# Tiled fp32 products become one entry of the schedule, and the planner charges tiling changes and strided operands

## The chip, the core and the metric

The kernel runs on one core of a Trainium2 chip. Of the core's engines this case needs TensorE (PE in the profile, with its weight loads apart as PEld), VectorE (DVE), ScalarE (ACT), GpSimd (POOL) and the queue SP that issues the DMAs. All of them run at once and meet at semaphores. The metric is the device time of one execution in microseconds; lower is better.

## The reference, cut to what matters

A two-layer encoder trunk on 512 tokens of width 1024, in float32. Each layer has four token mixers side by side, then a gated MLP with a short convolution:

```
h = rms_norm(x, attn_norm_g[i])
u_s5, conv_in, q_lat, kv_lat, k_pe, q_g, k_g, v_g = split(h @ w_in[i])
y_s5   = s5_mixer(u_s5, ...)        # two-way diagonal complex scan, 16 groups of 16 channels, state 64
y_conv = conformer_conv(conv_in)    # GLU, depthwise conv of 31 taps, LayerNorm, swish
y_mla  = mla_mixer(q_lat, kv_lat, k_pe, ...)   # 4 heads of 64, softmax over 512 keys
y_gqa  = gqa_mixer(q_g, k_g, v_g, ...)         # 4 heads of 64, 2 key/value heads
x = x + rms_norm(stack(y_s5, y_conv, y_mla, y_gqa)) @ w_out[i]
h = rms_norm(x, ffn_norm_g[i])
u = depthwise_conv3(h @ w_up[i]); gate, up = split(u)
x = x + (silu(gate) * up) @ w_down[i]
```

After both layers a last `rms_norm` gives the output.

## The kernel before

Activations lie transposed: channels on the 128 partitions, the 512 tokens along the free axis. Large products are taken in three passes of `fp32r` (a high and a low half of each operand; `mm3`, `product`); small ones are plain `fp32`, which takes two PE instructions for one product. Weights come by DMA, and DVE and ACT split them into halves.

The order of the work is not the order of the code. Every call on `V`, `A`, `T`, `X`, `GP` is put by `add` into a list of operations with their operands, and `_Plan.run` makes a schedule of that list: it walks a model of the five engines (`forward`), gives each operation a cost in ns from `_cost`, a delay between engines from `LAT`, and takes for each idle engine the ready operation of the highest priority whose buffers fit (51 `s` slots, 22 `b` slots, 16 `t` slots in SBUF, and the 8 banks of PSUM). Ten passes (`PASSES`) alternate with a backward walk that sets new priorities; the pass with the shortest model span is kept. `emit` then issues each operation in that order, so each engine's program is a fixed sequence. A copy (`copy`) may go to ACT or DVE; the walk decides. ACT holds one set of function tables at a time, and the walk takes `SWITCH` off the priority of an operation that needs another set.

All instructions are issued from one line of `emit`, L536, and table loads from L534, so the profile's groups have to be read by shape and operand names, not by line. In those names `bank` is a PSUM bank, `v_s`, `v_b`, `v_t` are SBUF slots, `c_sb` holds constants (the identity for transposes, a matrix of ones for sums), `xs__65` is the residual stream.

Four places use PE in column tiles: two or four products with 64 or 32 output columns run side by side in the array, each writing its own partitions of one bank. They go through `plan.tiled`, which takes the list of products of one row of tiles and enters them as one operation (a "group"); its cost is the largest of the row's products plus 53 ns for each further one. Below, "row" is one such set of tiles that run side by side.

- `s5_prep`, the kernel of the scan: 4 rows of two 64-column tiles, 128 moving columns, for each of 4 quarters and 2 layers (32 rows). Layer 1's run beside layer 0's MLP.
- `s5_out`, the output of the scan: 6 rows of the same kind for each of 4 quarters and 2 layers (48 rows).
- `attend`, probabilities times values: 4 rows of two 64-column tiles, 512 moving columns, for each of 4 pairs of heads and 2 layers (32 rows).
- `conv`, the depthwise convolution on PE: 4 rows of four 32-column tiles, 512 moving columns, 2 for each of 3 channel blocks (24 rows).

That is 136 rows, 136 operations, and the walk is free to put any other PE work between two rows. Where it does, PE changes its tiling. `_cost` knows nothing of that.

Of the kernel before, what the change touches and what calls it, by code (L numbers as in the profile page):

```python
# [17 lines left out]
P = 128  # L18
D = 1024
S = 512  # L20
# [91 lines left out]
class _Op:  # L112
    __slots__ = ("idx", "alts", "outs", "ins", "deps", "succ", "ndep", "ready", "rank", "bias", "boost", "eng", "done", "t0", "bufs")
# [9 lines left out]
class _Plan:  # L123
# [49 lines left out]
    def add(self, alts):  # L173
        op = _Op()
        op.idx, op.alts = len(self.ops), alts
# [7 lines left out]
        deps = set()  # L183
# [19 lines left out]
    def tiled(self, mms):  # L203

        d = max(_cost("T", *m)[4] for m in mms) + 53.0 * (len(mms) - 1)
        return self.add([("T", "group", mms, {}, d, 0.0, 0.0)])
# [103 lines left out]
    def forward(self, prio, ref, home, horizon):  # L310
# [9 lines left out]
        n = len(ops)  # L320
# [34 lines left out]
        act_set = self.LOG  # L355
        head = 0
# [46 lines left out]
        while len(order) < n:  # L403
            progress = False
            for e in free:
# [3 lines left out]
                for l in (("V", "F") if e == "V" else (e,)):  # L409
                    tries = 0  # L410
                    for z in cand[l]:
                        k = -z[0]
                        if bk is not None and k <= bk:
                            break
                        if e == "A":
                            st = self.act_of(z[3])
                            if st is not None and act_set not in st:
                                k -= self.SWITCH
                                if bk is not None and k <= bk:
                                    continue  # L420
                        if tries > self.TRIES and z[2] is not ops[ref[head]]:
                            continue
                        got = fits(z[2])
                        if got is not None:
                            best, bk, bg = z, k, got
                        else:
                            tries += 1
# [32 lines left out]
                dur = al[4]  # L460
                if e == "A":
# [41 lines left out]
    LAT = {("A", "V"): 140.0, ("V", "V"): 127.0, ("T", "V"): 196.0, ("T", "A"): 197.0, ("V", "A"): 200.0,  # L503
# [4 lines left out]
    SWITCH = 4000.0  # L508
    BETA = 40.0
# [46 lines left out]

def _cost(e, fn, a, k):
# [9 lines left out]
    elif e == "V":  # L567
# [13 lines left out]
        else:  # L581
            d = 68.0 + 1.04 * n
    elif e == "A":
# [5 lines left out]
        if "accum_out" in k:  # L589
            d += 90.0  # L590
    elif e == "G":
# [8 lines left out]
def trunk_kernel(  # L600
# [167 lines left out]
    def s5_prep(l, bias=0.0):  # L768
# [150 lines left out]
        for q4 in range(4):  # L919
# [38 lines left out]
            for pr in range(2):  # L958
                for c_ in range(2):
                    plan.tiled([("matmul", (kp[64 * e:64 * e + 64, pr], bm[:, c_, 2 * pr + e, :], gri[c_][:, 2 * pr + e]),  # L960
                                 {"start": c_ == 0, "stop": c_ == 1}) for e in range(2)])
# [76 lines left out]
    def s5_out(l, U, st):  # L1038
# [3 lines left out]
        for hf in range(2):  # L1042
            o_, p_ = ps((P, 4, P)), ps((P, 8, NC_))
            for q4 in range(2):
# [6 lines left out]
                for pr in range(2):  # L1051
                    for i in range(3):
                        plan.tiled([("matmul", (
                            o_[64 * e:64 * e + 64, 2 * q4 + pr],
                            U[:, 8 * hf + 4 * q4 + 2 * pr + e, :] if i == 0 else st[hf][:, i - 1, 4 * q4 + 2 * pr + e, :],
                            w_[i][:, 2 * pr + e, :]), {"start": i == 0, "stop": i == 2}) for e in range(2)])
# [59 lines left out]
    def attend(scores, vt):  # L1116
# [22 lines left out]
        for kb in range(4):  # L1139
            plan.tiled([("matmul", (o_[64 * hh:64 * hh + 64], vt[hh][:, kb, :], pt[hh][kb // 2][:, kb % 2, :]),  # L1140
                         {"start": kb == 0, "stop": kb == 3}) for hh in range(2)])
# [29 lines left out]
    def mixing(l):  # L1171
# [174 lines left out]
        def conv():  # L1346
            cv = []
            o, ot = VEC["dw_w"][0], VEC["dw_t"][0]
            for j in range(2):
# [22 lines left out]
                for gg in range(2):  # L1372
# [3 lines left out]
                    for f_ in range(4):  # L1376
                        plan.tiled([("matmul", (p_[32 * i:32 * i + 32], wt[:, 4 * i + f_, gg, :], win[i][:, f_:f_ + S]),
                                     {"start": gg + f_ == 0, "stop": gg + f_ == 4}) for i in range(4)])
# [337 lines left out]
```

## Time and profile before

| what | value |
|---|---|
| device time, median of 3 runs | 1236.8 us (1235.83, 1236.8, 2334.42) |
| device time of the profiled execution | 1235.14 us |
| its span, first to last instruction | 1233.1 us |
| granted TensorE clock, mean | 0.993 |
| instructions | 19808 |
| HBM read and written | 118.96 MB and 13.89 MB, 108 GB/s over the span |

The run at 2334.42 us stands alone; the other two and the profiled one agree within 0.2%. By time the program falls into the mixers of layer 0 (until about 225 us), its MLP (until about 620 us, with the first products of layer 1 in its last part), the mixers of layer 1 (until about 830 us) and its MLP. A busy time of PE in the profile counts a matmul from its start to a modelled end, so PE can be "busy" while its array waits; the starts of the matmuls are what shows its pace.

### The profile page before, as it was taken

The page shows a single profiled execution, that of the slowest core. Times are in us where ns is not written, and L with a number is a line of the kernel's source. Part 1 is how long each engine was busy: PE and PEld are TensorE (multiplying, and loading weights), DVE is VectorE, ACT ScalarE, POOL GpSimd, SP SyncE. Part 2 cuts the span into 40 slices and gives each one's busy share as a digit, 9 for nine tenths or more (in the row PEclk, how much of TensorE's full clock was granted, in tenths as well). Part 3 has the DMA queues.
Part 4 walks back from the last instruction along what each step waited for, and adds up shares of the span by engine and source line. Part 5 has one row for each costly group of instructions (what it writes and reads, how often), then busy time and mean ns, then how long its engine had stood idle before and what let it go on. Part 6 is the DMA issues. An engine that isn't in the chain of part 4 may idle for free.

```text
span 1233.1 us, 19808 instructions
## 1 busy us (share of the span) xinstructions
PE 1193.4 (97%) x7144; PEld 974.5 (79%) x7144; DVE 1122.9 (91%) x2204; ACT 718.1 (58%) x1366; POOL 6.9 (1%) x27
## 2 busy tenths in 40 slices
PE   7999999999999999979999999999999799999996
PEld 5874455778999998968878736558899799999996
DVE  8999988879999999999997997996899998999876
ACT  6348599446647566645463266883656454656543
POOL 0000000000000000000000000000000000000000
PEclk9999999999999999999999999999999999999998
DMA  8469582302333333314584164622124332333202
GB/s 320 137 215 270 118 218 78 112 1 86 103 95 102 105 95 109 98 61 144 188 283 121 35 148 91 181 77 70 46 89 131 94 103 91 107 101 111 89 1 69
DMA packets 88962, 144.64 MB, mean 117 GB/s; under 512 B 22176, under 2 KB 34976, under 8 KB 88736
## 3 DMA queue, kind: packets, MB, share of 16 engines
q1 hardware_dynamic: 88864, 143.38, 38.2%
q8 instruction: 56, 0.92, 0.3%
q14 instruction: 42, 0.34, 0.1%
HBM read 118.96 MB, written 13.89 MB: 108 GB/s over the span
## 4 chain that ended last, share of the span: by engine, by line
PE 77%; DVE 14%; ACT 4%; DMA 2%; issue 2%; SPq 1%; DVEq 0%; ACTq 0%
PE bank L536 77%; DVE v_s L536 11%; ACT v_s L536 3%; DVE v_b L536 2%; ACT v_b L536 1%; DVE v_t L536 1%; SPq L536 1%; DMA v_s<-y_d 0%; DMA v_s<-in_w_up_dram 0%; DMA y_d<-v_b 0%; ACT L534 0%; DMA v_b<-in_w_in_dram 0%; DVE xs__65 L536 0%; DMA v_b<-k_d 0%; DVEq L1711 0%
## 5 line engine op out<-in xcount | busy, mean ns | idle before, releaser
L536 PE MATMUL bank<-v_b,v_s 128*128 128x256 f32 (+3 forms) x3382 | 576.2, 293 | 4.3 <-DVE v_b L536 3.8
L536 PEld LDWEIGHTS bank<-v_b,v_s 128*128 128x128 f32 (+1 forms) x3382 | 478.1, 188 | 29.4 <-issue 7.2
L536 DVE TENSOR_TENSOR v_s<-v_s,v_s 128x512 fp32r<-128x512 f32 (+6 forms) x691 | 431.0, 654 | 12.7 <-ACT v_s L536 7.3
L536 PE MATMUL bank<-v_s,v_s 128*128 128x512 f32 (+2 forms) x1492 | 434.9, 378 | 2.4 <-DVE v_s L536 1.8
L536 PE MATMUL bank<-v_s,v_b 128*128 128x512 f32 (+3 forms) x1465 | 353.6, 416 | 12.1 <-ACT v_b L536 8.3
L536 PEld LDWEIGHTS bank<-v_s,v_s 128*128 128x128 f32 (+1 forms) x1492 | 254.1, 184 | 60.4 <-issue 9.9
L536 PEld LDWEIGHTS bank<-v_s,v_b 128*128 128x128 f32 (+2 forms) x1465 | 221.0, 173 | 94.5 <-issue 33.9
L536 ACT CAST v_s<-v_s 128x512 fp32r<-128x512 f32 (+2 forms) x387 | 224.2, 603 | 106.0 <-DVE v_s L536 77.2
L536 PE MATMUL bank<-v_b,v_b 128*128 128x256 f32 (+6 forms) x365 | 109.4, 408 | 6.7 <-DVE xs__65 L536 5.0
L536 ACT ACTIVATE v_s<-v_s 128x512 f32<-128x512 f32 (+2 forms) x121 | 69.6, 586 | 72.2 <-DVE v_s L536 71.5
L536 ACT ACTIVATE v_s<-bank 128x256 f32<-128x256 f32 x146 | 55.5, 384 | 84.8 <-PE bank L536 82.5
L536 DVE TENSOR_TENSOR xs__65<-xs__65,bank 128x512 f32<-128x512 f32 x120 | 80.4, 681 | 25.8 <-PE bank L536 25.6
L536 DVE SCALAR_TENSOR_TENSOR v_s<-v_s,vec__67,v_s 128x511 f32<-128x511 f32 (+7 forms) x130 | 95.8, 742 | 2.5 <-DMA v_s<-y_d 1.5
L536 PEld LDWEIGHTS bank<-v_b,v_b 128*128 128x128 f32 (+3 forms) x365 | 54.5, 175 | 28.7 <-issue 11.2
L536 DVE TENSOR_TENSOR v_b<-v_b,v_b 128x1024 fp32r<-128x1024 f32 (+5 forms) x74 | 75.7, 1035 | 1.0 <-ACT v_b L536 0.9
L536 ACT CAST v_b<-v_b 128x1024 fp32r<-128x1024 f32 (+3 forms) x57 | 53.6, 948 | 33.9 <-DVE v_b L536 10.4
L536 PEld LDWEIGHTS bank<-c_sb,v_s 128*128 128x128 f32 x360 | 43.5, 142 | 30.0 <-issue 18.1
L536 PE MATMUL bank<-c_sb,v_s 128*128 128x128 f32 x360 | 61.2, 279 | 3.1 <-ACT v_s L536 1.9
L536 ACT ACTIVATE v_s<-v_s,vec__67 128x512 f32<-128x512 f32 x51 | 41.3, 814 | 31.7 <-DVE v_s L536 31.5
L536 DVE TENSOR_TENSOR v_s<-v_b,v_s 128x128 f32<-128x128 f32 (+4 forms) x109 | 54.9, 521 | 2.0 <-ACT v_b L536 1.2
L536 DVE SCALAR_TENSOR_TENSOR v_s<-v_s,nfw__68,v_s 128x511 f32<-128x511 f32 x66 | 49.2, 745 | 3.4 <-ACT v_s L536 3.2
L536 DVE TENSOR_TENSOR v_s<-v_s,bank 128x256 f32<-128x256 f32 x109 | 44.6, 414 | 8.3 <-PE bank L536 7.3
(107 smaller groups left out, 802.0 us busy)
## 6 DMA issues: line engine op xcount, KB each, us to landing
v_s<-in_w_up_dram SPq DMA_DIRECT2D x164, 256.0 KB
v_b<-in_w_in_dram SPq DMA_DIRECT2D x28, 512.0 KB
v_s<-in_w_dn_dram SPq DMA_DIRECT2D x50, 256.0 KB
v_b<-in_w_out_dram SPq DMA_DIRECT2D x16, 384.0 KB
v_b<-v_b SPq DMA_DIRECT2D x24, 256.0 KB
v_s<-x_d SPq DMA_DIRECT2D x21, 257.5 KB
v_s<-in_w_dn_dram SPq DMA_DIRECT2D x26, 192.0 KB
v_s<-wt_d SPq DMA_DIRECT2D x16, 256.0 KB
```

Of the source, the lines that this page charges most:

```text
L536: self.issued(op, getattr(eng[e], fn)(*[res(z) for z in a], **{n: res(z) for n, z in k.items()}))
```

## The change

It has four parts, all in what the planner is told.

1. `tiled` takes a list of rows and enters them as one operation. The loops over rows in `s5_prep`, `s5_out`, `attend` and `conv` become lists handed over in one call, so that the 136 rows are 30 operations: 8 of 4 rows, 8 of 6, 8 of 4 and 6 of 4. Their cost is the sum over rows of the largest product in each; the 53 ns for each further tile are gone. An operation of several rows is placed when the operands of all its rows are ready.
2. The walk keeps the tiling in force on PE (`tiles`). An operation with another tiling loses `RETILE` (1000) of its priority, and is charged 175 ns when it is taken.
3. `_cost` charges a DVE operation of 64 elements and more 0.7 ns for each element if an operand's innermost stride is not 0 or 1 (`_broken`), and an ACT operation 95 ns for such an operand or for an output of under 128 partitions.
4. The delay from DVE to ACT in `LAT` goes from 200 to 130 ns.

What is computed, the buffers and the DMAs stay the same; every engine's order is planned anew.

```diff
-    def tiled(self, mms):
-
-        d = max(_cost("T", *m)[4] for m in mms) + 53.0 * (len(mms) - 1)
-        return self.add([("T", "group", mms, {}, d, 0.0, 0.0)])
+    def tiled(self, rows):
+
+        d = sum(max(_cost("T", *m)[4] for m in mms) for mms in rows)
+        op = self.add([("T", "group", [m for mms in rows for m in mms], {}, d, 0.0, 0.0)])
+        op.tiles = len(rows[0])
+        return op
...
+        tiles = 1
...
+                        if e == "T" and z[2].tiles != tiles:
+                            k -= self.RETILE
+                            if bk is not None and k <= bk:
+                                continue
...
                 dur = al[4]
+                if e == "T" and op.tiles != tiles:
+                    dur += 175.0
+                    tiles = op.tiles
...
-    LAT = {("A", "V"): 140.0, ("V", "V"): 127.0, ("T", "V"): 196.0, ("T", "A"): 197.0, ("V", "A"): 200.0,
+    LAT = {("A", "V"): 140.0, ("V", "V"): 127.0, ("T", "V"): 196.0, ("T", "A"): 197.0, ("V", "A"): 130.0,
...
+    RETILE = 1000.0
...
+def _broken(z):
+
+    if not isinstance(z, _Ap):
+        return False
+    dims = [d for d in list(z.proto.ap)[1:] if d[1] > 1]
+    return bool(dims) and dims[-1][0] not in (0, 1)
...
+        if n >= 64 and any(_broken(z) for z in a):
+            d += 0.7 * n
...
+        if a[0].shape[0] < P or any(_broken(z) for z in a):
+            d += 95.0
...
-            for pr in range(2):
-                for c_ in range(2):
-                    plan.tiled([("matmul", (kp[64 * e:64 * e + 64, pr], bm[:, c_, 2 * pr + e, :], gri[c_][:, 2 * pr + e]),
-                                 {"start": c_ == 0, "stop": c_ == 1}) for e in range(2)])
+            plan.tiled([[("matmul", (kp[64 * e:64 * e + 64, pr], bm[:, c_, 2 * pr + e, :], gri[c_][:, 2 * pr + e]),
+                          {"start": c_ == 0, "stop": c_ == 1}) for e in range(2)] for pr in range(2) for c_ in range(2)])
...
-        for kb in range(4):
-            plan.tiled([("matmul", (o_[64 * hh:64 * hh + 64], vt[hh][:, kb, :], pt[hh][kb // 2][:, kb % 2, :]),
-                         {"start": kb == 0, "stop": kb == 3}) for hh in range(2)])
+        plan.tiled([[("matmul", (o_[64 * hh:64 * hh + 64], vt[hh][:, kb, :], pt[hh][kb // 2][:, kb % 2, :]),
+                      {"start": kb == 0, "stop": kb == 3}) for hh in range(2)] for kb in range(4)])
```

The calls in `s5_out` and `conv` change in the same way. In the changed program the issuing line is L547 and table loads stand at L545.

Three places show what moves. The first is PE in the mixers of layer 0, before: rows of `s5_out` (output `64x128`, one printed row a row of tiles) alternate with products of other work (`128x512`).

```order
L536 MATMUL bank4_76<-v211_s10_1277,v252_b16_1512 64x128 x2
L536 MATMUL bank5_77<-v263_b9_1575,v49_b13_295 128x512
L536 MATMUL bank4_76<-v213_s12_1285,v252_b16_1512 64x128 x2
L536 MATMUL bank5_77<-v250_s33_1502,v61_b21_358 128x512
L536 MATMUL bank4_76<-v216_s43_1300,v83_b12_475 64x128 x2
L536 MATMUL bank0_72<-v267_s11_1599,v74_s32_429 128x512
L536 MATMUL bank4_76<-v211_s10_1277,v252_b16_1512 64x128 x2
L536 MATMUL bank2_74<-v238_b4_1450,v243_s16_1474 128x512
L536 MATMUL bank4_76<-v213_s12_1285,v252_b16_1512 64x128 x2
L536 MATMUL bank0_72<-v253_s30_1514,v81_s36_466 128x512
```

The same work on PE in the changed program:

```order
L547 MATMUL bank5_77<-v214_b8_1265,v223_s8_1326 128x512
L547 MATMUL bank1_73<-v237_s7_1432,v88_b17_521 64x128 x2
L547 MATMUL bank1_73<-v233_s44_1420,v270_b0_1602 64x128 x2
L547 MATMUL bank1_73<-v218_s18_1297,v270_b0_1602 64x128 x2
L547 MATMUL bank1_73<-v237_s7_1432,v88_b17_521 64x128 x2
L547 MATMUL bank1_73<-v233_s44_1420,v270_b0_1602 64x128 x2
L547 MATMUL bank1_73<-v218_s18_1297,v270_b0_1602 64x128 x2
L547 MATMUL bank3_75<-c_sb_63,v263_s38_1575 128x128
```

Six rows stand behind each other, with a change of tiling ahead and one behind, where before each row had both.

The second place is PE in the first attention of layer 0, before: the rows of `attend` (output `64x512`, two printed rows a row of tiles) have transposes (`c_sb`) or other products between them.

```order
L536 MATMUL bank2_74<-v338_b17_1876,v258_s47_1545 64x512
L536 MATMUL bank2_74<-v355_b14_1939,v258_s47_1545 64x512
L536 MATMUL bank3_75<-c_sb_63,v346_s21_1904 128x128
L536 MATMUL bank2_74<-v338_b17_1876,v258_s47_1545 64x512
L536 MATMUL bank2_74<-v355_b14_1939,v258_s47_1545 64x512
L536 MATMUL bank3_75<-c_sb_63,v346_s21_1904 128x128
L536 MATMUL bank2_74<-v339_b6_1881,v258_s47_1545 64x512
L536 MATMUL bank2_74<-v358_b7_1951,v258_s47_1545 64x512
L536 MATMUL bank0_72<-v290_b19_1687,v279_b1_1648 128x512
```

And in the changed program:

```order
L547 MATMUL bank7_79<-v307_b2_1753,v311_b16_1766 128x512
L547 MATMUL bank1_73<-v325_b0_1857,v242_s39_1468 64x512
L547 MATMUL bank1_73<-v328_b9_1863,v242_s39_1468 64x512
L547 MATMUL bank1_73<-v325_b0_1857,v242_s39_1468 64x512
L547 MATMUL bank1_73<-v328_b9_1863,v242_s39_1468 64x512
L547 MATMUL bank1_73<-v329_b15_1867,v242_s39_1468 64x512
L547 MATMUL bank1_73<-v336_b1_1895,v242_s39_1468 64x512
L547 MATMUL bank1_73<-v329_b15_1867,v242_s39_1468 64x512
L547 MATMUL bank1_73<-v336_b1_1895,v242_s39_1468 64x512
L547 MATMUL bank3_75<-v339_s28_1919,c_sb_63 128x512
```

The transposes that stood between the rows have gone ahead of them or behind them.

The third place is ACT near the end of the attention of layer 0, before: the last loads of function tables there stand three operations apart, around one tanh (`v8_t4_148` is its bias) and one swish (`vec__67`).

```order
L536 ACTIVATE v443_s49_2269,v392_t3_2077<-bank4_76,v438_t1_2243 128x512
L534 ACT_TABLE_LOAD
L536 ACTIVATE v445_s46_2276<-bank2_74,v8_t4_148 128x512
L536 ACTIVATE v446_s36_2284<-v257_s13_1536,vec__67 128x512
L534 ACT_TABLE_LOAD
L536 ACTIVATE v448_s18_2292,v392_t3_2077<-bank1_73,v440_t10_2257 128x512
```

In the changed program the swish stands later and has a pair of loads of its own:

```order
L545 ACT_TABLE_LOAD
L547 ACTIVATE v450_s18_2347<-v250_s2_1497,vec__67 128x512
L547 CAST v455_s36_2358<-v451_s5_2350 128x512
L547 ACTIVATE v456_s23_2360<-v450_s18_2347 128x512
L547 CAST v459_s47_2367<-v406_s42_2180 128x512
L547 CAST v460_s37_2372<-v410_s28_2195 128x512
L547 CAST v461_s33_2376<-v362_s46_2005 128x256
L547 CAST v462_s44_2381<-v371_s12_2035 128x256
L547 CAST v463_s21_2384<-v394_s35_2123 128x512
L547 ACTIVATE v467_s27_2394<-v443_s4_2320 128x512
L547 CAST v470_s2_2402<-v427_s7_2263 128x512
L545 ACT_TABLE_LOAD
```

Over the whole program ACT has 25 table loads where it had 22, and 5 copies more, which DVE has less. On PE, the changes of tiling in the order are 56 where they were 229: 28 for 113 in the mixers of layer 0, 8 for 26 in the rows of `s5_prep` for layer 1, 20 for 90 in the mixers of layer 1.

More of the change, by code (lines that the diff above doesn't have):

```diff
@@ L112 @@
 class _Op:
-    __slots__ = ("idx", "alts", "outs", "ins", "deps", "succ", "ndep", "ready", "rank", "bias", "boost", "eng", "done", "t0", "bufs")
+    __slots__ = ("idx", "alts", "outs", "ins", "deps", "succ", "ndep", "ready", "rank", "bias", "boost", "eng", "done", "t0", "bufs", "tiles")
 def _free(ap):
@@ L174, in add @@
         op = _Op()
-        op.idx, op.alts = len(self.ops), alts
+        op.idx, op.alts, op.tiles = len(self.ops), alts, 1
         op.outs, op.ins = [], []
@@ L1050, in s5_out @@
                     X.dma_start(w_[1 + c_], g_d[c_][2 * hf + q4].rearrange("p (g e) -> p g e", g=4))
[L1051 to L1056, printed above, removed]
+                plan.tiled([[("matmul", (
+                    o_[64 * e:64 * e + 64, 2 * q4 + pr],
+                    U[:, 8 * hf + 4 * q4 + 2 * pr + e, :] if i == 0 else st[hf][:, i - 1, 4 * q4 + 2 * pr + e, :],
+                    w_[i][:, 2 * pr + e, :]), {"start": i == 0, "stop": i == 2}) for e in range(2)]
+                    for pr in range(2) for i in range(3)])
             z = s2(shape=(P, 4, P))
@@ L1375, in conv @@
                         X.dma_start(win[i], x_d[j].window([[XW, 16], [4, 8], [1, S + 3]], XW * (32 * i + 16 * gg)))
-                    for f_ in range(4):
-                        plan.tiled([("matmul", (p_[32 * i:32 * i + 32], wt[:, 4 * i + f_, gg, :], win[i][:, f_:f_ + S]),
-                                     {"start": gg + f_ == 0, "stop": gg + f_ == 4}) for i in range(4)])
+                    plan.tiled([[("matmul", (p_[32 * i:32 * i + 32], wt[:, 4 * i + f_, gg, :], win[i][:, f_:f_ + S]),
+                                  {"start": gg + f_ == 0, "stop": gg + f_ == 4}) for i in range(4)] for f_ in range(4)])
                 acc = s2()
```

## The prediction, made before the changed kernel ran

> **What bounds the kernel now.** I read the page's first two parts, then the chain of work that ended last, then what PE's weight loads waited for, then the stretches of the two mixer stages.
>
> ```profile
> PE 1193.4 (97%) x7144; PEld 974.5 (79%) x7144; DVE 1122.9 (91%) x2204; ACT 718.1 (58%) x1366; POOL 6.9 (1%) x27
> PE 77%; DVE 14%; ACT 4%; DMA 2%; issue 2%; SPq 1%; DVEq 0%; ACTq 0%
> ```
>
> The first row gives busy time, share of the span and instructions of each engine, the second the shares of the chain. PE carries the kernel and DVE is close behind. The work of PE doesn't change: 7144 instructions before, and as many follow from the new order. So the time can only come out of PE's pauses. Next, what the weight loads waited for (total us, times, longest), and below it the same for two stretches, 120 to 151 us and 720 to 764 us:
>
> ```profile
> PEld bank L536 <- issue: 80.7, 242, 1.1
> ...
> PEld bank L536 <- issue: 14.6, 53, 0.8
> ...
> PEld bank L536 <- issue: 16.7, 50, 1.1
> ```
>
> "issue" is waiting for nothing that the profile shows. It happens 242 times, and the order on PE has 229 changes of tiling. The two stretches hold 40 and 53 of these changes by the order, set against the starts in the trace. The 80.7 us are not the loss itself, since weight loads run beside matmuls; its size is read from the starts of the matmuls below. The stretches, with busy time of PE, PEld, DVE and ACT:
>
> ```profile
> 75.00:225.00 150.00, 146.63 (x846) 86.41 (x846) 136.06 (x303) 114.03 (x241) 2.00 (x7) 1.00 0.62 172
> 225.00:525.00 300.00, 299.54 (x1933) 271.40 (x1933) 288.00 (x573) 177.47 (x327) 0.72 (x3) 1.00 0.29 91
> 650.00:825.00 175.00, 170.33 (x876) 109.88 (x875) 155.23 (x327) 106.18 (x206) 0.49 (x4) 0.99 0.39 101
> 84.00:120.00 36.00, 35.25 (x204) 21.24 (x202) 35.23 (x112) 25.45 (x59) 1.01 (x5) 1.00 0.97 283
> 120.00:151.00 31.00, 30.51 (x220) 13.67 (x221) 28.34 (x67) 17.15 (x36) 0.00 (x0) 1.00 0.52 118
> 701.00:720.00 19.00, 16.39 (x72) 10.62 (x72) 18.87 (x68) 7.99 (x15) 0.24 (x2) 1.00 0.09 28
> 720.00:764.00 44.00, 44.00 (x260) 23.23 (x261) 39.30 (x67) 30.06 (x64) 0.00 (x0) 0.96 0.53 124
> ```
>
> In the mixers PE looks busy (146.6 of 150 us) although weights load for only 86.4 us; in the MLP of layer 0 they load for 271.4 of 300. The mixers are where PE pauses under cover of its busy time, and where nearly all the tiled rows are.
>
> **The price of a change of tiling.** The timeline of PE (start, time, instruction, count) at four places: a steady stream, a row of two 64-column tiles with 128 moving columns, one with 512, and a run of 32-column tiles without a change.
>
> ```profile
> 59.67 1.09 PE L536 MATMUL bank<-v_s,v_b 128*128 128x512 f32 x4
> 60.60 0.33 PE L536 MATMUL bank<-v_b,v_b 128*128 128x64 f32 x2
> ...
> 145.41 0.50 PE L536 MATMUL bank<-v_b,v_s 128*128 128x512 f32 x1
> 145.84 0.44 PE L536 MATMUL bank<-v_s,v_b 128*64 128x128 f32 x4
> 146.21 0.51 PE L536 MATMUL bank<-v_s,v_s 128*128 128x512 f32 x1
> ...
> 166.27 1.08 PE L536 MATMUL bank<-v_b,v_s 128*64 128x512 f32 x4
> 167.28 0.33 PE L536 MATMUL bank<-c_sb,v_s 128*128 128x128 f32 x1
> 167.54 1.08 PE L536 MATMUL bank<-v_b,v_s 128*64 128x512 f32 x4
> ...
> 169.82 0.44 PE L536 MATMUL bank<-c_sb,v_s 128*128 128x128 f32 x2
> ...
> 120.49 2.35 PE L536 MATMUL bank<-v_s,v_b 128*32 128x512 f32 x20 [1.24 <-ACT v_s L536]
> ```
>
> Steady, four 512-column matmuls take 60.60 - 59.67 = 0.93 us, 0.23 each. Ahead of a tiled row the same matmul takes 145.84 - 145.41 = 0.43, so going in costs 0.20. The row takes 0.37 until the next matmul starts. Its own work I take from the run: 20 instructions are five passes of four tiles; less the last one's length (about 0.6) they take 1.75, 0.44 a pass of 512 columns, 0.11 for 128, 0.22 for the row's two passes. Coming out costs 0.15. The 512-column row takes 1.01 until the transpose, 0.13 over its 0.88, and that transpose 0.26 where two stand 0.11 apart (0.44 less 0.33), 0.15 over. So a change costs 0.14 to 0.175 us. I take 0.15, since about half of the changes are exits, whose price lies at the low end. The run also shows that rows behind each other cost nothing extra.
>
> The Trainium skill, "TensorEngine Tiling (Array Packing)", section "Key Properties", says that changing the tiling mode drains TensorE. The trace agrees only in part: at 145.84 the tiled row starts 0.07 us before the matmul of 145.41 + 0.50 has ended by the profile. By the rule to the letter going in would cost 0.27, and 173 changes at that price would be 47 us; the trace's start times decide for the smaller price.
>
> **The change part by part.** *Rows as one entry.* 229 changes become 56, 173 less. At 0.15 us that is 26.0 us of PE (24.2 to 30.3 by the two ends). What of it lies on the path? The chain in order of time (start, us, what):
>
> ```profile
> 120.49 30.22 PE bank L536 x218
> ...
> 163.85 8.60 PE bank L536 x48
> ...
> 188.63 1.28 ACT L534
> ...
> 198.86 132.62 PE bank L536 x685
> ...
> 571.02 105.72 PE bank L536 x570
> ...
> 719.87 43.76 PE bank L536 x254
> ```
>
> Set against the starts in the trace, 163 of the 229 changes lie in stretches in which the chain is PE's: 8 at 74 to 84, 40 at 120 to 151, 8 at 164 to 172, 16 at 198 to 225, 24 at 552 to 678, 53 at 720 to 764, 14 at 796 to 830. The other 66 lie where DVE, ACT or a transfer carries the chain, 31 of them at 84 to 120, where DVE is busy 35.2 of 36 us. So 163/229 of 26.0, 18.5 us, comes off directly. Of the other 7.5 I take half, 3.7: the plan is free to move PE's saved time, but DVE has only 14 us left in 75 to 225 and covers part of it.
>
> *Waiting for all operands.* Four rows of `attend` could start as the transposes went on; now three more of them, 3 x 0.88 = 2.6 us, come after the last copy. Where other PE work stands by, that costs nothing, and at 198.86 the chain has 132.62 us of PE without a break. At worst it is paid at the end of both attentions, 5.3 us. I take 0. A long entry also holds PE up to 3.5 us (4 x 0.88, `conv`) against something urgent; the run at 120.49 did so before, so 0.
>
> *Table loads.* Three more at 1.28 us. One stands by the order near the end of layer 0's attention, where ACT carries the chain (188.63), so +1.3; the others lie in the second layer, where ACT is busy 30.1 of 44 us. Ends 0 and 3.8.
>
> *Costs of strided operands, the delay of 130, copies.* They change only the order. DVE loses 5 copies, some 0.6 us each by the chain's steps, and ACT gains them. In 225 to 525 PE is busy 299.5 of 300 us and DVE 288.0, so I take 0; ends -3 and 0. That a plan with truer prices also has fewer waits isn't priced; it goes into the range.
>
> Sum: -18.5 - 3.7 + 1.3 = -20.9. The profiled execution took 1235.14 us (span 1233.1 and 2.0 around it), so it would be 1214.2; the median is 1.7 above that execution, so 1215.9, say 1216.
>
> **The rivals.**
>
> ```profile
> PE bank L536 <- ACT v_b L536: 9.4, 3, 8.3
> PE bank L536 <- DVE v_b L536: 6.6, 4, 3.8
> ...
> PE bank L536 <- DVE xs__65 L536: 5.0, 1, 5.0
> ...
> PEld bank L536 <- ACT v_s L536: 17.0, 30, 2.1
> PE bank L536 <- DVE v_b L536: 2.4, 1, 2.4
> 975.00:980.00 5.00, 0.03 (x1) 0.00 (x0) 5.00 (x10) 2.80 (x5) 0.00 (x0) 0.97 0.62 191
> ```
>
> *More than the changes.* Besides 8.3 us at the start, PE has two long waits on DVE, 3.8 and 5.0. They come from how the old order met the chip; nothing ties them to the work. If all 26.0 us pay and these two go, it is 1236.8 - 26.0 - 8.8 = 1202. For it: the old plan priced the rows wrongly, so its engines met at other moments than planned. Against: DVE is busy the whole 5.0 us of the second wait.
>
> *DVE takes over, or new waits give it back.* DVE has 35.2 of 36 us at 84 to 120 and 18.9 of 19 at 701 to 720. If the planner's saved PE time only turns into waits on DVE through both mixers, the part outside the chain (7.5) and half of the rest (9.3) are lost: 26.0 - 7.5 - 9.3 - 1.3 = 8 off, about 1229; with one new wait of the kind seen (5.0) 1234. For it: DVE's 91%. Against: DVE pauses in the same stages as PE, 14 us in the first mixers and 20 in the second, so it isn't full there.
>
> *Slower.* The 30 entries each hold PE's queue until their last operand is there, and all products behind stand still. The weight loads wait 0.57 us a time on ACT (17.0 / 30). At that price 30 entries cost 17 us and the time is 1216 + 17 = 1233. From 0.70 us an entry (20.9 / 30) the gain is gone, from 1.5 us (20.9 + 24.7 = 45.6 over 30) it is slower by 2%. Against: the planner knows of these operands, and the single wait of 5.0 us in the row above is as rare as it is long.
>
> The clock adds to it: it was granted at 0.97 in 975 to 980 and 0.96 in 720 to 764, beside waits of PE of 5.0 us and of 2.4 (the row ahead of the last, from 678 to 720 us). The Trainium skill, "TensorE: Matmul & The Clock Gate", section "Part 1: The HAM clock gate", has a rule for it: after an idle window of about 3.4 us TensorE runs at half its clock until it has been busy as long. By that, a new wait above 3.4 us costs some 1.7 us more, an estimate from that page; the trace's mean of 0.96 over 44 us, 1.8 us lost, agrees in size, though the wait ahead of it was shorter than that window.
>
> **How the numbers follow.** Within 2% is about what a measurement of this kernel can tell from no change; here 1212.1 to 1261.5. The changes pay as summed, 1208 to 1223: 0.55. More than that, 1197 to 1208: 0.16. Given back, 1223 to 1245: 0.24, in which 1236.8 has its place. Slower by over 2%: 0.05. Faster by over 2% are the second case and the lower part of the first, 0.16 + 0.20 = 0.36; slower 0.05; the rest, 0.59, is within 2%. The predicted time is the likeliest case's, 1216. The range: from 1200, just under the 1202 of all changes paid and both long waits gone, to 1239, the 1234 of the DVE case with one more wait of 5; it leaves out about 2 in 10.
>
> **What would show it.** Right: weight loads wait on "issue" some 60 to 80 times instead of 242; matmuls in the tiled runs step by 0.43 to 0.44 us a pass; the mixers end earlier by 10 us in layer 0 and by 20 in all after layer 1, while the MLPs keep their length. Wrong: a count of issue waits as low as that and yet DVE at 97% through the mixers, with waits of PE on DVE that grew by what the changes gave up; or long PE waits ahead of the first matmul of a tiled run, on ACT or a transfer; or a clock below 0.9 in a slice of a mixer stage. A time below 1205 would say that the new order also closed waits that had nothing to do with tiling.

## The result, and the profile after

The changed kernel takes 1219.41 us (median of 4 runs, 1218.68 to 1220.42), the kernel before 1235.83 beside it. The ratio is 0.9866, 95% interval 0.9847 to 0.9885: 16.4 us less, a change of under 2%. The forecast was 1216. (A run of some double time stood beside two kernels, 2334.42 us beside before and 2332.71 beside e4_costs; both are left out of the medians here, which with them would be 1236.32 and 1246.42.) The profiled execution of the changed kernel took 1220.42 us, its span is 1218.6, 14.5 less than before's 1233.1.

Two rows of its page, busy time by engine and the shares of the chain, to set against those of before:

```profile
PE 1171.7 (96%) x7144; PEld 982.5 (81%) x7144; DVE 1118.5 (92%) x2199; ACT 725.1 (60%) x1374; POOL 7.0 (1%) x27
...
PE 69%; DVE 22%; DMA 3%; ACT 3%; issue 2%; SPq 0%; DVEq 0%; ACTq 0%
```

PE has the same 7144 instructions and is busy 21.7 us less: pauses that counted as busy are gone (14.5 us of span) or stand as idle time now (46.9 us where it was 39.7). DVE's share of the chain rose from 14% to 22%. The waits of the changed kernel (total us, times, longest):

```profile
PEld bank L547 <- issue: 53.1, 169, 1.7
...
PEld bank L547 <- DVE xs__65 L547: 15.4, 4, 5.9
PE bank L547 <- DVE xs__65 L547: 14.4, 3, 5.8
PEld bank L547 <- ACT v_s L547: 14.1, 22, 1.6
...
PE bank L547 <- ACT v_b L547: 9.4, 3, 7.9
```

Waiting for nothing fell from 80.7 to 53.1 us, but from 242 times to 169 only, though the order has 56 changes of tiling where it had 229. The long waits of before on `v_b` (3.8 us) are not there; three waits on the residual additions (`xs__65`) stand here, 14.4 us in all, for one of 5.0 before.

The stretches of the changed kernel, columns as before (the last three numbers are the clock, the DMA share and GB/s):

```profile
475.00:525.00 50.00, 38.43 (x250) 34.94 (x249) 46.32 (x81) 19.32 (x39) 0.53 (x1) 0.86 0.26 80
75.00:225.00 150.00, 145.17 (x885) 95.81 (x884) 142.67 (x315) 116.44 (x245) 2.06 (x7) 0.99 0.61 180
225.00:525.00 300.00, 288.15 (x1845) 260.45 (x1844) 285.74 (x567) 168.70 (x313) 1.25 (x4) 0.98 0.27 86
...
650.00:825.00 175.00, 170.29 (x928) 122.49 (x927) 165.72 (x344) 118.88 (x226) 0.49 (x4) 0.99 0.49 135
```

In both mixer stretches more work goes through in the same time: PE has 885 instructions where it had 846, and 928 where it had 876; DVE is busy 142.7 us where it was 136.1, and 165.7 where it was 155.2. (The second pair is no clean comparison: the changed kernel is ahead by then, so the same 175 us hold later work.) In 225 to 525 PE loses what it had, 288.2 us busy for 299.5, all of it after 475, where it is busy 38.4 of 50.

The end of the mixers shows the size of the gain. The first number of time in each row is when the first of the 16 residual additions of the stage starts. After, in layer 0 and in layer 1 (two answers of one view):

```profile
L547 DVE TENSOR_TENSOR xs__65<-xs__65,bank x16: 681/689/692, 211.0 to 252.8; 128x512 f32<-128x512 f32 x16
...
L547 DVE TENSOR_TENSOR xs__65<-xs__65,bank x16: 680/687/694, 817.3 to 850.9; 128x512 f32<-128x512 f32 x16
```

And before:

```profile
L536 DVE TENSOR_TENSOR xs__65<-xs__65,bank x16: 675/677/689, 222.1 to 263.1; 128x512 f32<-128x512 f32 x16
...
L536 DVE TENSOR_TENSOR xs__65<-xs__65,bank x16: 675/683/689, 826.1 to 866.6; 128x512 f32<-128x512 f32 x16
```

Layer 0's mixers end 11.1 us earlier by the first addition. The second layer's end only 8.8 earlier by the first addition, 15.7 by the last: the MLP of layer 0 gave part of it back.

To see where PE gains and loses I summed, for every matmul of a trace, the time to the start of the next one less a steady price, which is an estimate from the usual steps in the traces (0.23 us for 512 columns, 0.12 for 256, 0.11 for 128, 0.21 for an instruction of a tiled pass of 512), in us. The absolute numbers move by some us with these prices, the differences between kernels by about 1. The last three columns are experiments told below.

| stretch | before | after | e1_gather | e2_spread | e12_boost |
|---|---|---|---|---|---|
| 75 to 225, mixers of layer 0 | 30.2 | 19.4 | 29.4 | 28.5 | 22.9 |
| 475 to 525 | 1.8 | 19.0 | 1.8 | 15.6 | 1.1 |
| 525 to 600 | 15.1 | 3.9 | 14.1 | 9.5 | 2.3 |
| 700 to 825, mixers of layer 1 | 25.0 | 13.9 | 26.8 | 19.1 | 16.7 |
| all other time | 34.5 | 35.4 | 32.7 | 36.3 | 38.0 |
| sum | 106.6 | 91.6 | 104.8 | 109.0 | 81.0 |

The sums differ as the spans do, to within 0.6 us: 15.0 less after, 14.5 by the span. The change won 10.8 and 11.1 us in the two mixers and gave 6.0 back at 475 to 600 (22.9 where 16.9 was lost before).

What it gave back stands mainly in two waits. PE's timeline of the changed kernel, as in the prediction:

```profile
497.42 0.41 PE L547 MATMUL bank<-v_b,v_b 128*128 128x64 f32 x2 [0.64 <-issue]
497.67 0.39 PE L547 MATMUL bank<-v_s,v_b 128*128 128x64 f32 x2
503.85 0.69 PE L547 MATMUL bank<-v_b,v_b 128*128 128x64 f32 x2 [5.79 <-DVE xs__65 L547]
504.33 0.63 PE L547 MATMUL bank<-v_s,v_b 128*128 128x64 f32 x2
...
519.20 1.01 PE L547 MATMUL bank<-v_b,v_s 128*128 128x256 f32 x3 [3.63 <-DVE xs__65 L547]
```

And DVE's of the same kernel at the first of them:

```profile
498.29 4.90 DVE L547 TENSOR_TENSOR v_s<-v_s,v_s 128x512 f32<-128x512 f32 x8
503.11 1.88 DVE L547 TENSOR_TENSOR xs__65<-xs__65,bank 128x512 f32<-128x512 f32 x3
```

PE's next product needs a PSUM bank that a residual addition has to empty. DVE does eight other additions first, 4.90 us of them, and then three residual additions in a row; PE goes on at 503.85, when the first of these is through.

### The profile page after: what moved, and what is told of

The parts are those of the page before. It is cut to its first block, busy times and chain, and to the rows that moved or that the text cites. A ratio compares the mean times of both kernels' runs of the same rounds, so it can differ in the third digit from the quotient of the medians.

```text
span 1218.6 us, 19786 instructions
## 1 busy us (share of the span) xinstructions
PE 1171.7 (96%) x7144; PEld 982.5 (81%) x7144; DVE 1118.5 (92%) x2199; ACT 725.1 (60%) x1374; POOL 7.0 (1%) x27
## 4 chain that ended last, share of the span: by engine, by line
PE 69%; DVE 22%; DMA 3%; ACT 3%; issue 2%; SPq 0%; DVEq 0%; ACTq 0%
PE bank L547 69%; DVE v_s L547 16%; DVE v_b L547 5%; ACT v_s L547 2%; DVE v_t L547 1%; DMA v_s<-wt_d 1%; DMA v_s<-y_d 1%; ACT L545 1%; ACT v_b L547 0%; DMA v_s<-v_b 0%; DMA v_s<-in_w_up_dram 0%; DMA y_d<-v_b 0%; DVE xs__65 L547 0%; DMA v_b<-in_w_in_dram 0%; SPq L547 0%
## 5 line engine op out<-in xcount | busy, mean ns | idle before, releaser
L547 PE MATMUL bank<-v_b,v_s 128*128 128x256 f32 (+3 forms) x3382 | 577.4, 294 | 13.1 <-DVE xs__65 L547 8.6
L547 PEld LDWEIGHTS bank<-v_b,v_s 128*128 128x128 f32 (+1 forms) x3382 | 484.6, 189 | 45.9 <-issue 13.1
L547 DVE TENSOR_TENSOR v_s<-v_s,v_s 128x512 fp32r<-128x512 f32 (+6 forms) x713 | 446.9, 660 | 18.0 <-ACT v_s L547 8.6
L547 PE MATMUL bank<-v_s,v_s 128*128 128x512 f32 (+2 forms) x1418 | 410.1, 377 | 2.9 <-DVE v_s L547 2.0
L547 PE MATMUL bank<-v_s,v_b 128*128 128x512 f32 (+3 forms) x1497 | 360.5, 410 | 8.6 <-ACT v_b L547 7.9
L547 ACT CAST v_s<-v_s 128x512 fp32r<-128x512 f32 (+2 forms) x388 | 225.0, 602 | 129.1 <-DVE v_s L547 76.6
L547 PEld LDWEIGHTS bank<-v_s,v_b 128*128 128x128 f32 (+2 forms) x1497 | 233.1, 174 | 74.2 <-issue 14.8
L547 PEld LDWEIGHTS bank<-v_s,v_s 128*128 128x128 f32 (+1 forms) x1418 | 242.8, 184 | 55.0 <-issue 6.5
L547 PE MATMUL bank<-v_b,v_b 128*128 128x256 f32 (+6 forms) x407 | 106.9, 396 | 8.0 <-DVE xs__65 L547 5.8
L547 ACT ACTIVATE v_s<-v_s 128x512 f32<-128x512 f32 (+2 forms) x120 | 69.0, 585 | 73.2 <-DVE v_s L547 72.6
L547 ACT ACTIVATE v_s<-bank 128x256 f32<-128x256 f32 x148 | 56.5, 383 | 76.1 <-PE bank L547 75.2
L547 DVE SCALAR_TENSOR_TENSOR v_s<-v_s,vec__67,v_s 128x511 f32<-128x511 f32 (+15 forms) x125 | 92.6, 747 | 4.0 <-DMA v_s<-y_d 2.2
L547 DVE TENSOR_TENSOR xs__65<-xs__65,bank 128x512 f32<-128x512 f32 x120 | 80.9, 685 | 16.1 <-PE bank L547 16.1
L547 PEld LDWEIGHTS bank<-v_b,v_b 128*128 128x128 f32 (+3 forms) x407 | 60.7, 173 | 28.6 <-issue 13.2
L547 DVE TENSOR_TENSOR v_b<-v_b,v_b 128x1024 fp32r<-128x1024 f32 (+4 forms) x67 | 73.5, 1111 | 0.7 <-PE bank L547 0.3
L547 ACT CAST v_b<-v_b 128x1024 fp32r<-128x1024 f32 (+3 forms) x62 | 58.0, 946 | 22.6 <-PE bank L547 10.3
L547 PE MATMUL bank<-c_sb,v_s 128*128 128x128 f32 x364 | 64.6, 281 | 3.8 <-ACT v_s L547 1.8
L547 PEld LDWEIGHTS bank<-c_sb,v_s 128*128 128x128 f32 x364 | 45.1, 144 | 18.2 <-ACT v_s L547 5.1
L547 ACT ACTIVATE v_s<-v_s,vec__67 128x512 f32<-128x512 f32 x49 | 39.7, 814 | 33.7 <-DVE v_s L547 31.2
L547 DVE TENSOR_TENSOR v_s<-v_s,bank 128x256 f32<-128x256 f32 x112 | 46.4, 418 | 13.9 <-PE bank L547 13.3
L547 DVE SCALAR_TENSOR_TENSOR v_s<-v_s,nfw__68,v_s 128x511 f32<-128x511 f32 x68 | 50.9, 749 | 3.4 <-ACT v_s L547 3.2
L547 ACT ACTIVATE v_s<-bank,v_t 128x512 f32<-128x512 f32 x66 | 45.2, 691 | 10.9 <-DVE v_t L547 10.3
```

The lines of the kernel that those rows point to most:

```text
L547: self.issued(op, getattr(eng[e], fn)(*[res(z) for z in a], **{n: res(z) for n, z in k.items()}))
```

## The experiments

Two readings stand against each other. The prediction's: the changes of tiling lie on the path, and taking them away gives their time back, whatever the plan. The rival: PE is not alone on the path, DVE and ACT stand right behind it, and what is gained comes from the plan as a whole. Kernels e1, e2, e4 and e5 take the parts of the change one by one; e3 and e12 look at the wait that appeared; the others vary one number of the planner each.

**e1_gather: only the changes of tiling, in the old order.** The kernel before, its plan left as it was; then each row of tiles is moved to the place of the last row of the same product, where the buffers allow it. The order has 58 changes where it had 229.

```diff
+    def gather(self):
...
+        for g in groups.values():
+            i = 0
+            while i < len(g):
+                k = len(g) - 1
+                while k > i and not all(limit(z) > pos[g[k]] for z in g[i:k]):
+                    k -= 1
+                for z in g[i:k]:
+                    moved[z] = pos[g[k]]
+                i = k + 1
+        key = {op: (moved.get(op, i), i) for op, i in pos.items()}
+        self.order = sorted(order, key=key.get)
```

> The schedule of before, not planned anew: only, the rows of one product that stood apart on PE are issued together at the place of their last row. 229 changes of tiling become 58, nothing else moves. Theory A (the changes themselves are the gain, 0.15 us each, some 70 to 85% of it on the path): 171 x 0.15 = 25.7 us less on PE, time 1214 to 1220. Rival B (the gain comes from the plan with truer prices, the changes were hidden): 1231 to 1237. Rival C (DVE is the bound beside them and takes half or more of it): 1224 to 1230.

Measured: 1234.36 us, ratio 0.9994 (0.9984 to 1.0004), 1.0 us less. 171 changes are gone and almost nothing is gained. What its weight loads wait for, and the stretches of the two mixers:

```profile
PEld bank L589 <- issue: 58.0, 179, 1.1
PEld bank L589 <- ACT v_s L589: 32.0, 32, 7.7
```

```profile
75.00:225.00 150.00, 137.91 (x841) 89.83 (x840) 136.66 (x306) 115.34 (x244) 2.00 (x7) 0.98 0.63 174
650.00:825.00 175.00, 159.68 (x871) 110.75 (x870) 155.91 (x330) 105.16 (x209) 0.49 (x4) 0.97 0.37 99
```

The pauses went: the wait for nothing fell by 22.7 us, PE is busy 8.7 and 10.7 us less in the two mixers. But no more PE instructions get through (841 and 871, before 846 and 876), and DVE and ACT do what they did. The weight loads' wait on ACT rose by 15.0 us instead. One place shows it. PE of e1_gather at the depthwise convolution:

```profile
113.58 0.59 PE L589 MATMUL bank<-v_s,v_b 128*32 128x512 f32 x1
118.07 8.93 PE L589 MATMUL bank<-v_s,v_b 128*32 128x512 f32 x66 [3.90 <-ACT v_s L589]
126.42 0.59 PE L589 MATMUL bank<-v_b,v_b 128*32 128x512 f32 x1
```

And of before:

```profile
118.65 0.60 PE L536 MATMUL bank<-v_s,v_b 128*32 128x512 f32 x2
120.49 7.49 PE L536 MATMUL bank<-v_s,v_b 128*32 128x512 f32 x66 [1.24 <-ACT v_s L536]
127.40 0.59 PE L536 MATMUL bank<-v_b,v_b 128*32 128x512 f32 x1
```

Before, PE reaches the run of 66 after 118.65 and waits 1.24 us for ACT. Gathered, it is there about 5 us earlier, waits 3.90, starts 2.4 us earlier, and a lower clock (the last section has it) takes another part: the 66 instructions need 8.35 us instead of 6.91. At 127 us the two stand 1.0 us apart. In the chain this place belonged to PE (30.22 us from 120.49), and so did the 40 changes in it; ACT was 1.24 us away.

**e2_spread: the changes put back into the new order.** The changed kernel; after planning, the rows of an entry are issued with neighbouring full-array products between them. The order has 216 changes where it had 56.

```diff
+            for i, r in enumerate(rows):
+                seq.append((g, r))
+                if i < len(back):
+                    seq.append(back[i])
...
+        self.order = [z for op in order for z in out[op]]
```

> The schedule of after, not planned anew: only, the rows of an entry are issued with the neighbouring full-array products between them. 56 changes of tiling become 216. Theory A: 160 x 0.15 = 24 us more on PE, 70 to 85% of it on the path, time 1219.4 + 17 to 20 = 1236 to 1240. Rival B (the new plan is better whatever the changes): 1219 to 1224. Rival C: 1226 to 1232.

Measured: 1238.56 us, 1.0022 (1.0012 to 1.0032), 19.1 us over the changed kernel (1238.56 - 1219.41). Its two mixers, and two waits of its weight loads over the whole run:

```profile
75.00:225.00 150.00, 145.70 (x843) 85.62 (x843) 134.17 (x301) 112.36 (x239) 2.07 (x7) 1.00 0.57 161
650.00:825.00 175.00, 173.22 (x906) 115.85 (x905) 153.10 (x321) 111.63 (x213) 0.49 (x4) 1.00 0.49 133
...
PEld bank L615 <- issue: 74.1, 210, 0.8
...
PEld bank L615 <- ACT v_s L615: 11.1, 20, 1.4
```

160 changes cost 19.1 us, 0.12 each: in the new order most of the prediction's price of 0.14 to 0.175 is paid. The full-array products that moved between the rows count in that too, but they brought no new waits on other engines that the profile shows: the wait for nothing rose by 21.0 us (74.1 - 53.1), that on ACT fell from 14.1 to 11.1. PE is busy as long as before with less in it (weight loads 85.6 us for 95.8), and DVE falls back from 142.7 to 134.2. So changes of tiling have two effects here: in the old order they stood mostly in the place of waits that were due anyway, in the new one they are on the path. The Trainium skill, "TensorEngine Tiling (Array Packing)", section "Key Properties", says that changing the tiling mode drains TensorE; the 0.12 us a change agree with it in kind.

**e4_costs and e5_rows: the two halves of the change.** e4_costs is the kernel before with the strided prices and the delay of 130, rows single (211 changes). e5_rows is the changed kernel without the strided prices and with the delay of 200 (48 changes).

```diff
-        if n >= 64 and any(_broken(z) for z in a):
-            d += 0.7 * n
...
-        if a[0].shape[0] < P or any(_broken(z) for z in a):
-            d += 95.0
```

(That is e5_rows, beside the delay; e4_costs adds the same lines to the kernel before.)

> Before with the prices of strided operands and the delay of 130 ns alone; rows are entries of their own as before, 211 changes of tiling in the order. Theory A: no gain from these beyond 18 changes less (2.7 us) and the scatter of a new plan, 1226 to 1244. Rival B: these prices carry the gain, 1215 to 1224.

> After without the prices of strided operands and with the old delay of 200 ns; rows in one entry and the price of a change stay, 48 changes of tiling in the order. Theory A: the gain stays, 1211 to 1228 with the scatter of a new plan. Rival B: 1231 to 1242.

Measured: e4_costs 1244.76 us, 1.0079 (1.0053 to 1.0105), above both of its ranges; e5_rows 1236.57 us, 1.0017 (0.9997 to 1.0036). Neither half gains anything in the one plan that each of these is, and together they gain 16.4. Why e4_costs is 9.4 us slower than before (1235.38 beside it) stays open; plans scatter by as much (below).

**e3_notap: is the new wait DVE's load?** The changed kernel, in whose layer 0 the third tap of the MLP's short convolution is left out: 44 operations of DVE, some 26 us.

```diff
+                if op.skip:
+                    continue
...
-            V.scalar_tensor_tensor(y[:, 0:S - 1], u[:, 1:S], cw(2), y[:, 0:S - 1], ALU.mult, ALU.add)
+            V.scalar_tensor_tensor(y[:, 0:S - 1], u[:, 1:S], cw(2), y[:, 0:S - 1], ALU.mult, ALU.add).skip = l == 0
```

> The schedule of after, with 44 DVE operations left out as they are issued: the third tap of the short convolution in layer 0's MLP (26 us of DVE by steps of 0.6 us), so that part of the result is not computed. Theory D (DVE carries layer 0's MLP, and the PE waits of 6.0 and 3.8 us at 498 to 519 us are DVE's): these waits go, time 1219.4 - 8 to 12 = 1207 to 1212. Rival (they hang on a chain of single operations, not on DVE's load): 1216 to 1220.

Measured: 1216.86 us, 0.9845 (0.983 to 0.9859), 2.5 us less than the changed kernel for 26 us less of DVE's work. What PE waits for in 475 to 600, and DVE at the wait:

```profile
PE bank L549 <- DVE xs__65 L549: 7.9, 2, 5.1
```

```profile
497.39 5.50 DVE L549 TENSOR_TENSOR v_s<-v_s,v_s 128x512 f32<-128x512 f32 x9
502.81 1.88 DVE L549 TENSOR_TENSOR xs__65<-xs__65,bank 128x512 f32<-128x512 f32 x3
```

Both waits stay, 7.9 us where they were 9.4. DVE's load over the whole MLP is not what makes them: nine other operations still stand ahead of the three residual additions in DVE's fixed order.

**e8_nostride, e11_dveonly, e7_lat200, e6_noretile: the planner's numbers, one by one.** Each is the changed kernel with one thing taken back: all strided prices; ACT's 95 ns alone; the delay; the loss of priority and the 175 ns for a change of tiling.

```diff
-        if n >= 64 and any(_broken(z) for z in a):
-            d += 0.7 * n
...
-        if a[0].shape[0] < P or any(_broken(z) for z in a):
-            d += 95.0
...
-    LAT = {("A", "V"): 140.0, ("V", "V"): 127.0, ("T", "V"): 196.0, ("T", "A"): 197.0, ("V", "A"): 130.0,
+    LAT = {("A", "V"): 140.0, ("V", "V"): 127.0, ("T", "V"): 196.0, ("T", "A"): 197.0, ("V", "A"): 200.0,
...
-                    dur += 175.0
+                    dur += 0.0
...
-    RETILE = 1000.0
+    RETILE = 0.0
```

(e8 has the first two hunks, e11 the second, e7 the third, e6 the last two.)

> After without the prices of strided operands, the delay at 130, all else as in after; 58 changes. If the strided prices carry what the run without both lost: 1231 to 1240. If the delay carries it: 1215 to 1224. Theory S: anywhere from 1215 to 1245.

> After with the strided price on DVE alone, the 95 ns on ACT left out. Theory P1 (the plan has to know DVE's true time in the scan): 1216 to 1227. Theory P2 (it is ACT's price): 1232 to 1240, like the plans without strided prices (1236.6, 1237.9).

> After with the old delay of 200 ns from DVE to ACT, all else as in after; 54 changes. If the strided prices carry what the run without both lost: 1215 to 1224. If the delay carries it: 1231 to 1240. Theory S: anywhere from 1215 to 1245.

> After with RETILE at 0 and no 175 ns for a change of tiling; rows in one entry and the prices of strided operands and the delay of 130 stay; 53 changes in the order. Theory D1 (the plan must know the price of a change to fill PE): 1228 to 1240. Theory D2 (rows in one entry and true prices of DVE and ACT are enough): 1215 to 1224. Theory S (the plan's scatter decides): anywhere from 1215 to 1245.

**e9_beta39 and e10_beta41: how far plans scatter.** BETA, the weight of the program's own order in the first priorities, is 40. Changing it by one has nothing to do with tiling or strides.

```diff
-    BETA = 40.0
+    BETA = 39.0
```

(e10 has 41.0.)

> After with one number of the planner moved by a hair, BETA 39 for 40, which means nothing for the work but gives another order (58 changes of tiling). Theory P (rows in one entry together with the strided prices make the gain): 1216 to 1227, like the two other plans with both (1223.9, 1224.7). Theory S (a plan's scatter is as large as the gain): anywhere from 1215 to 1245.

> After with BETA 41 for 40 (51 changes of tiling), a second neutral plan. Theory P: 1216 to 1227. Theory S: anywhere from 1215 to 1245. Both of these within 1216 to 1227 speak for P, one above 1230 for S.

Measured, all with their rows in one entry, sorted by time:

| kernel | changes | DVE's strided price | us | ratio to before, interval |
|---|---|---|---|---|
| e9_beta39 | 58 | yes | 1218.62 | 0.986, 0.9845 to 0.9874 |
| changed kernel | 56 | yes | 1219.41 | 0.9866, 0.9847 to 0.9885 |
| e11_dveonly | 58 | yes | 1222.03 | 0.9886, 0.9871 to 0.9901 |
| e6_noretile | 53 | yes | 1223.9 | 0.9912, 0.9889 to 0.9936 |
| e7_lat200 | 54 | yes | 1224.72 | 0.9907, 0.9884 to 0.9931 |
| e10_beta41 | 51 | yes | 1228.75 | 0.9941, 0.9925 to 0.9958 |
| e5_rows | 48 | no | 1236.57 | 1.0017, 0.9997 to 1.0036 |
| e8_nostride | 58 | no | 1237.88 | 1.0018, 0.9999 to 1.0036 |

Six plans with DVE's strided price lie between 1218.6 and 1228.8, the two without it at 1236.6 and 1237.9. Two neutral plans stand 10.1 us apart (1228.75 - 1218.62), the slower one above its range for P, so nothing can be said of the delay, of ACT's 95 ns or of the loss of priority: taking them back moves the time by 2.6 to 5.3 us, less than that scatter. Taking back DVE's price costs more than the scatter: e8_nostride is 15.9 us behind e11_dveonly, which has only that price more, and e5_rows 11.9 behind e7_lat200, which has the strided prices more. These are two plans, and both lie on the same side of the six others, though only 7.8 us from the nearest (1236.57 - 1228.75). Were the price without effect, the two without it would come last of eight in 1 case of 28. So the price's effect is likely, but it rests on two plans.

Where the gap lies: the stretches of both mixers of e8_nostride.

```profile
75.00:225.00 150.00, 138.43 (x848) 91.14 (x846) 135.91 (x307) 114.97 (x239) 2.07 (x7) 0.98 0.62 171
...
650.00:825.00 175.00, 167.77 (x892) 117.86 (x890) 154.11 (x318) 112.09 (x215) 0.49 (x4) 0.98 0.46 127
```

And of e11_dveonly, which differs in DVE's price alone:

```profile
75.00:225.00 150.00, 144.12 (x878) 94.54 (x878) 144.79 (x325) 116.51 (x240) 2.06 (x7) 1.00 0.62 184
...
650.00:825.00 175.00, 166.52 (x909) 118.32 (x908) 161.84 (x339) 114.90 (x226) 0.48 (x4) 0.97 0.48 129
```

With the price DVE gets more work done in both stretches. But e11_dveonly is ahead of e8_nostride when the second begins, so that pair holds different work. The residual additions on DVE tell the stages apart. The table has the start of three of them, and the span, in us:

| kernel | layer 0, end of mixers (first) | layer 0, end of MLP (last) | layer 1, end of mixers (first) | span |
|---|---|---|---|---|
| before | 222.1 | 631.6 | 826.1 | 1233.1 |
| e8_nostride | 225.3 | 636.9 | 831.4 | 1235.3 |
| e11_dveonly | 217.4 | 621.9 | 819.9 | 1220.6 |
| changed kernel | 211.0 | 628.0 | 817.3 | 1218.6 |
| e9_beta39 | 216.6 | 619.2 | 812.1 | 1216.2 |
| e7_lat200 | 227.1 | 626.2 | 822.0 | 1222.9 |

The whole lead of e11_dveonly over e8_nostride, 15.0 us, is there at the end of layer 0, about half of it (7.9) from its mixers; the second mixers add nothing. The other plans with both parts got their gain at other places: e9_beta39, the fastest of the table, wins half of what the changed kernel wins in layer 0's mixers (5.5 us to 11.1), and e7_lat200 is 5.0 us later than before there and still 10.2 shorter in the end. So the total goes with the price in these plans, and the stage in which it is won doesn't.

That the price has the right size can be read from the groups of before, kept apart by shape: operations of 128 elements on DVE that read the scan's buffers (`v_b`, by the program most often with a stride) and those that don't.

```profile
L536 DVE TENSOR_TENSOR v_s<-v_b,v_s 128x128 f32<-128x128 f32 x49 | 17.6, 389 | 1.2 <-ACT v_b L536 1.2
...
L536 DVE TENSOR_TENSOR v_s<-v_s,v_s 128x128 f32<-128x128 f32 x21 | 5.7, 282 | 0.0
```

389 - 282 = 107 ns for 128 elements, 0.84 for each, where the change charges 0.7. By which step of the plan the truer price helps wasn't followed, and stays open.

**e12_boost: the residual additions first.** If it is DVE's order that makes the new wait, putting these additions first should take it away: the changed kernel with more priority for them.

```diff
-                V.tensor_add(x[m], x[m], p_)
+                V.tensor_add(x[m], x[m], p_).boost = 4000.0
```

(at both places, `mixers` and `blocks`.)

> After with 4000 more priority for the additions to the residual stream, which free the banks that PE waited for at 498 to 504, 515 to 519 and 958 to 964 us (6.0, 3.8 and 5.2 us). Theory Q (PE waits there because DVE's queue has other work ahead of these additions): the three waits shrink by half or more, time 1219.4 - 5 to 10 = 1209 to 1214. Rival (the new plan moves the waits elsewhere): 1217 to 1230.

Measured: 1212.92 us (1210.03 to 1213.93), 0.981 (0.9796 to 0.9825), below the changed kernel's interval. PE's waits in 475 to 600, all of them, and those on the residual additions over the whole run (two answers of one view):

```profile
PE bank L547 <- DVE v_b L547: 0.5, 1, 0.5
...
PE bank L547 <- DVE xs__65 L547: 4.7, 1, 4.7
```

The two waits of 5.8 and 3.6 us are gone; a third, in the second layer's MLP, stays. In the table of lost time the stretch 475 to 600 falls from 22.9 to 3.4, while the new plan loses 6.3 more in the two mixers: the plan was made anew for this too. (Its profiled execution, at 1210.03, is the fastest of its four.) It is the fastest of the kernels that were run. But its 6.5 us less than the changed kernel are under the scatter of neutral plans, and e9_beta39, without the boost, has no wait of PE above 1.5 us on a residual addition at 475 to 600 either. So this run agrees with the reading that DVE's order makes the wait, and doesn't show that the priority took it away; the reading itself stands on the timeline.

## Why the prediction was right in its number, and where not in its steps

*The price of a change: about right.* 0.14 to 0.175 us from the steps, of which I took 0.15; e2_spread pays 0.12 each for 160 of them. Tiled runs step as forecast. PE of the changed kernel in an attention:

```profile
156.49 3.65 PE L547 MATMUL bank<-v_b,v_s 128*64 128x512 f32 x16
160.07 1.97 PE L547 MATMUL bank<-c_sb,v_s 128*128 128x128 f32 x16
```

16 instructions are eight passes, 3.58 us until the next matmul, 0.45 a pass with the way in and out; 0.43 to 0.44 was forecast.

*"163/229 of 26.0, 18.5 us, comes off directly": wrong.* This step took a stretch in which the chain is PE's for a stretch in which only PE matters. In the old order e1_gather removes 171 changes and gains 1.0 us; only in the new order are the changes on the path (e2_spread). The chain names the engine that ended last; it doesn't say by how much, and ACT and DVE were close (1.24 us at 120.49). The profile had the sign: DVE 35.2 of 36 us at 84 to 120 and 91% over the run.

*"Costs of strided operands, the delay of 130, copies: 0": wrong in its largest part.* Without DVE's strided price the rows in one entry gain nothing (e5, e8). The text had it that a plan with truer prices "isn't priced". Both errors have about the same size and opposite signs: that the sum stood at 1216 is luck. It is luck of a second kind too, since neutral plans of the same change lie between 1218.6 and 1228.8. What the runs show in their place: six plans with rows gathered and DVE's price lie 6.8 to 16.9 us below before; two with the rows but not that price, and one with the prices but not the rows, gain nothing. In the changed kernel PE won 10.8 and 11.1 us in the two mixers, in other plans elsewhere.

*The half of 7.5 us outside PE's chain* can't be told apart from the rest any more, since the split by the chain doesn't hold.

*Waiting for all operands: 0 was forecast, and the slower rival priced it.* No such cost shows: the weight loads wait on ACT 14.1 us in 22 waits, before 17.0 in 30.

*Table loads.* Three more, as counted; no run tells their price.

*"New waits give it back"* was a rival with 5.0 us for one such wait, and it is what happened at 475 to 525: two waits, 5.8 and 3.6 us. It decided only part of the time, because 525 to 600 won 11.2 us (15.1 to 3.9), so that 6.0 us net were lost. The rival's reason, that DVE has too much work, isn't borne out by e3_notap, where 26 us less left the waits standing; the timeline points to DVE's order.

*The signs.* Mixers of layer 0 10 us earlier: 11.1 measured. 20 in all after layer 1: 8.8 to 15.7 measured, less by what 475 to 600 took, so that the MLP of layer 0 didn't keep its length. Issue waits at 60 to 80: 169 measured, and 179 in e1_gather; they aren't a count of changes of tiling, and a forecast by their number was no test of the path. A clock below 0.9 came where it wasn't looked for, in an MLP.

## What to carry to other kernels

A chain of waits says who ended last, not how much slack lies behind; before a stall on it is priced at its full length, look at what the next engine's waits at that place amount to, or take the stall away in the old order and see. Here the planner turned removed stalls into time only in plans that also had DVE's strided price, so a price change is best tested with and without the change it serves. Before a part of such a change is credited, measure how far neutral plans scatter (10 us here); and where a new wait on an engine appears, look at what stands ahead in its queue before lightening its load.

## What the hardware showed beyond that

A long wait of PE cost more than its length here. Behind the wait of 5.79 us the same pair of products steps by 0.48 us (503.85 to 504.33), where ahead of it it took 0.25 (497.42 to 497.67). The granted clock (the number after POOL's) of the changed kernel there:

```profile
498.00:504.00 6.00, 0.21 (x2) 0.15 (x1) 6.00 (x11) 1.72 (x4) 0.00 (x0) 0.75 0.07 27
504.00:507.50 3.50, 3.24 (x14) 2.84 (x15) 2.64 (x6) 0.53 (x1) 0.00 (x0) 0.50 0.01 2
...
519.00:523.00 4.00, 3.80 (x18) 3.81 (x19) 2.99 (x7) 1.31 (x3) 0.00 (x0) 0.50 0.20 66
```

Half speed for 3.5 us and for 4 us at least, so at least some 1.8 and 2.0 us on top of the waits' 5.8 and 3.6. In e1_gather it is 0.62 over the 4 us behind the wait of 3.90:

```profile
118.00:122.00 4.00, 3.93 (x24) 1.03 (x28) 3.94 (x15) 3.87 (x10) 0.00 (x0) 0.62 0.53 166
```

That is 1.5 us lost (0.38 x 4), as much as its run of 66 took longer (8.35 - 6.91 = 1.44), and before, with a wait of 1.24 us at this place, the clock was 1.00 over the same 4 us. So of the 2.4 us by which PE started the run earlier, 1.0 was left at its end. The Trainium skill, "TensorE: Matmul & The Clock Gate", section "Part 1: The HAM clock gate", has TensorE at half its clock after an idle window of about 3.4 us until it has been busy as long; the 0.50 over 3.5 us behind 5.79 us of waiting agrees.
